# A float32 decoder trunk on one core: S5 output weights staged by two k, four input-matrix buffers, a wide mLSTM gate projection, and two of four state sums left to TensorE

## The chip, the cores and the metric

The kernel runs on one NeuronCore of one Trainium2 chip. Such a core has TensorE (PE in the profile, its weight load PEld), VectorE (DVE), ScalarE (ACT), GpSimd (POOL) and SyncE (SP), whose queue issues most DMAs. Each engine executes its own instructions in the order in which they stand; engines wait for each other by semaphores. The metric is the device time of one execution in microseconds, lower is better. The kernel before takes 1262.76 us, the median of 3 runs (1262.62 to 1263.53).

## What is computed

The reference is a decoder trunk of 4 layers over one sequence of 256 tokens with 1024 channels, in float32. Each layer is a token mixer and a SwiGLU block, both with a residual and a layer norm after:

```python
for i in range(DEPTH):                       # DEPTH = 4
    kind = i % 3                             # 0 HGRN2, 1 mLSTM, 2 S5
    h = mixer[kind](x, ...)
    x = _layernorm(ALPHA * x + h, ln_g[i, 0], ln_b[i, 0])
    x = _layernorm(ALPHA * x + _swiglu(x, ffn_w_gate_up[i], ffn_w_down[i]), ln_g[i, 1], ln_b[i, 1])
```

The change touches the mLSTM mixer (layer 1) at its gates, and the S5 mixer (layer 2):

```python
# mLSTM: 16 gate columns (8 input gates, 8 forget gates) of the input projection
gates = (x @ w_in)[..., 2 * MLSTM_QK_W + 2 * D_MODEL:] + gate_b
# S5: 64 groups of 16 channels, each with a complex diagonal state of 64
u = x @ w_in
bu = einsum('blgc,gpc->blgp', u, bbar)       # complex
s[t] = abar * s[t-1] + bu[t]                 # complex, a scan over the tokens
y = einsum('blgp,gcp->blgc', s_re, c_re) - einsum('blgp,gcp->blgc', s_im, c_im) + d_skip * u
za, zb = split(gelu(y) @ w_out, 2)
return za * sigmoid(zb)
```

## The kernel before

**Two-term products.** Every float32 operand of a large product is held as a high part in float32r (`hi`, `xh`) and the rest (`lo`, `xl`), and a product is three matmuls: high by high, low by high, high by low (`mm3`). Activations lie in one tile `xx` whose two halves are `xh` and `xl`, 256 tokens each.

**Weight stages.** All weights come in stages of 128 partitions by up to 2048 columns (1 MB), in the order of a list (`plan`). `wstage` hands out the next stage and lets `stage_next` prepare the one after (AHEAD = 1). `stage_next` issues a stage's DMA into one of three buffers (tile `w`, line 108), then for each 1024 columns ScalarE makes the high part (line 129) and VectorE the low part (line 130), into one of eight `hi`/`lo` buffer pairs. `as_part` uses such units with tokens as the stationary side, `ws_block` (lines 176 to 182) with weights as the stationary side.

**The order.** The program is traced in the order of the source, and a scheduler at build time then puts each engine's instructions in an order by that priority and by its own idea of what is ready; a NoSync dependency added by hand forces an order on one engine without a semaphore.

**mLSTM gates.** `ml_gw` holds the 16 gate columns in a 128-wide block (8 at column 0, 8 at column 32, the rest zero). Line 713 multiplies it with `ws_block`: 8 slices of k, three matmuls over 256 columns each. Lines 721 and 722 add the gate bias out of PSUM. A chain of operations on 8 partitions follows; it ends in `mr` (line 735), which the first `head` reads on TensorE in line 777, after four `conv` blocks of matmuls.

**S5.** `s5_prepare` builds the tables (rotations `cs`, input matrices `bm`, output matrices `ch`, `cw`) inside the FFNs of layers 0 and 1 and writes them to DRAM (`table_out`). `s5` then runs through four pairs p of blocks, with three rotating working tiles `rot`:

- `project`, `project_part`, `land`: u = x @ w_in by quarters, transposed into place by VectorE
- `inputs(p)` (line 1158): TensorE applies `bm` to u; both blocks of a pair, 128 instructions. `bm` has two buffers, so a pair's matrices can be loaded when the previous `inputs` has read them
- `forth(p)` (lines 1161 to 1174): VectorE rotates the product, adds, and scans along the tokens in chunks of 64 with a real decay
- `back(p)` (lines 1176 to 1183): VectorE rotates the scan's result back: a product `x`, a product `y`, and their sum into the state tile `hs`, 64 values per chunk behind a zero in front (rows of 65)
- `outputs(p)`: TensorE adds the part within a chunk (`cw`, line 1197, 64 matmuls of 64 columns over all pairs) and the part of the state (`ch` by `hs`, line 1204) in PSUM, ScalarE applies GELU. The profile counts each of these float32 matmuls as two instructions: 64 of line 1204 for each pair
- `turn` (lines 1210 to 1219): transposes the result and splits it into `xh` and `xl` for two slices of k
- `few(n)`: takes n of the pieces that `turn` made available. A piece is one pair's share (two slices of k) of one of four output banks (token half h, column half i of `w_out`), 6 matmuls of 512 columns

A stage of `w_so` holds four slices of k for one column half i. So pair 0's four pieces need two stages. Columns 0 to 1023 of the output (n = 0) are made from pieces between the pairs; those of n = 1 follow with `out_part`, and `gated` and the layer norm end the mixer.

## Time and profile before

| | |
|---|---|
| median of 3 runs | 1262.76 us (1262.62 to 1263.53) |
| profiled execution, whole | 1263.76 us |
| its span, first to last instruction | 1262.0 us |
| mean granted TensorE clock | 0.996 |
| DMA over the span | 247.91 MB, 196 GB/s |
| S5 mixer, by the windows shown below | about 640 to 742 us of the span |

The page's first line gives each engine's busy time, its share of the span and its instructions. Matmuls are pipelined: one of 512 columns is busy for 0.40 us, but the next starts 0.23 us after it, so times of a series are read from starts. A number in brackets at the end of an instruction's line is the idle time of its engine ahead of it, with what ended it. The windows are in us from the span's start.

### The profile page before, as it was taken

What the parts mean: (1) busy time and instruction counts of PE and PEld (TensorE: products, weight loads), DVE (VectorE), ACT (ScalarE), POOL (GpSimd) and SP (SyncE); (2) the same over time, 40 slices, a digit from 0 to 9 for tenths busy, and PEclk for the clock granted to TensorE, in tenths of its full rate; (3) what the DMA queues carried; (4) which work ended last, traced back from release to release, by engine and by line L of the source; (5) the groups of instructions that cost most, each with busy time, mean ns of one, the idle gap of its engine ahead of it and who ended that gap; (6) DMA issues with size and microseconds to landing.
All of it is one profiled execution on the core that took longest, in us unless ns stands there. A gap on an engine that the chain in (4) does not pass through costs nothing.

```text
span 1262.0 us, 21505 instructions
## 1 busy us (share of the span) xinstructions
PE 1243.3 (99%) x8541; PEld 1038.9 (82%) x8541; DVE 958.1 (76%) x1703; ACT 704.6 (56%) x1144; POOL 36.2 (3%) x58
## 2 busy tenths in 40 slices
PE   9999999999999999999998999999999999999997
PEld 7977788888798888888886778888889878888886
DVE  6887899876787799866599787666586887766664
ACT  6755576565467555666443455555459654555551
POOL 0000000000100100000000000000000000000000
PEclk9999999999999999999999999999999999999999
DMA  8833466665374266656569546555545432745530
GB/s 310 299 135 134 169 219 230 251 228 200 102 278 148 100 249 237 240 201 224 185 240 337 192 165 248 187 200 179 188 156 217 169 132 95 276 173 194 190 144 34
DMA packets 46340, 247.91 MB, mean 196 GB/s; under 512 B 5504, under 2 KB 11024, under 8 KB 19872
## 3 DMA queue, kind: packets, MB, share of 16 engines
q1 hardware_dynamic: 46112, 246.46, 53.8%
q8 instruction: 67, 1.10, 0.4%
q14 instruction: 33, 0.27, 0.1%
q0 software_dynamic: 128, 0.09, 0.0%
HBM read 233.94 MB, written 12.58 MB: 195 GB/s over the span
## 4 chain that ended last, share of the span: by engine, by line
PE 91%; DVE 4%; DMA 2%; ACT 1%; issue 0%; SPq 0%; DVEq 0%; ACTq 0%
PE g L189 19%; PE g L159 10%; PE g L161 10%; PE g L192 10%; PE g L160 10%; PE a L160 9%; PE a L159 9%; PE a L161 9%; PE a L348 1%; PE t L250 1%; DMA ch<-s5ch 1%; DVE lo L130 1%; PE a L642 1%; DMA first<-in_first 1%; DMA w<-in_w_hg 1%; PE t L1048 1%
## 5 line engine op out<-in xcount | busy, mean ns | idle before, releaser
L130 DVE TENSOR_TENSOR lo<-w,hi 128x1024 fp32r<-128x1024 f32 x389 | 471.8, 1220 | 115.2 <-ACT hi L129 107.9
L129 ACT CAST hi<-w 128x1024 fp32r<-128x1024 f32 x389 | 406.2, 1050 | 201.0 <-PE a L160 112.9
L189 PE MATMUL g<-xx,hi 128*128 128x512 f32 x1024 | 358.2, 395 | 0.0
L192 PE MATMUL g<-xx,lo 128*128 128x256 f32 x1024 | 267.1, 281 | 0.0
L189 PEld LDWEIGHTS g<-xx,hi 128*128 128x128 f32 x1024 | 186.7, 188 | 34.5
L192 PEld LDWEIGHTS g<-xx,lo 128*128 128x128 f32 x1024 | 192.4, 188 | 10.3
L159 PE MATMUL g<-hi,xx 128*128 128x512 f32 (+1 forms) x416 | 167.5, 404 | 2.4 <-ACT xx L269 1.8
L161 PE MATMUL g<-lo,xx 128*128 128x512 f32 (+1 forms) x416 | 165.3, 399 | 0.1
L160 PE MATMUL g<-hi,xx 128*128 128x512 f32 (+1 forms) x416 | 164.7, 397 | 0.0
L329 ACT COPY sum<-g 128x256 f32<-128x256 f32 x128 | 47.6, 372 | 147.7 <-PE g L189 147.5
L159 PE MATMUL a<-hi,hh 128*128 128x512 f32 x328 | 129.4, 395 | 0.0
L161 PE MATMUL a<-lo,hh 128*128 128x512 f32 x328 | 129.2, 394 | 0.0
L160 PE MATMUL a<-hi,hl 128*128 128x512 f32 x328 | 128.8, 393 | 0.0
L330 DVE TENSOR_TENSOR sum<-g,sum 128x256 f32<-128x256 f32 x128 | 54.2, 423 | 69.2 <-ACT sum L329 68.6
L159 PEld LDWEIGHTS g<-hi,xx 128*128 128x128 f32 x416 | 78.3, 188 | 20.6 <-ACT xx L269 2.7
L161 PEld LDWEIGHTS g<-lo,xx 128*128 128x128 f32 x416 | 78.2, 188 | 18.9 <-DVE lo L130 2.1
L160 PEld LDWEIGHTS g<-hi,xx 128*128 128x128 f32 x416 | 78.3, 188 | 15.8
L161 PEld LDWEIGHTS a<-lo,hh 128*128 128x128 f32 x328 | 61.5, 188 | 14.5
L160 PEld LDWEIGHTS a<-hi,hl 128*128 128x128 f32 x328 | 61.5, 188 | 14.4 <-DVE hl L319 0.2
L159 PEld LDWEIGHTS a<-hi,hh 128*128 128x128 f32 x328 | 61.4, 188 | 12.6 <-ACT hh L318 0.2
L159 PE MATMUL g<-xx,hi 128*128 128x256 f32 x200 | 56.4, 282 | 0.9 <-DVE k L593 0.9
L160 PE MATMUL g<-xx,lo 128*128 128x256 f32 x200 | 56.5, 282 | 0.0
(299 smaller groups left out, 1758.0 us busy)
## 6 DMA issues: line engine op xcount, KB each, us to landing
w<-in_w_gu SPq DMA_DIRECT2D x88, 1024.0 KB, 4.8
w<-in_w_dn SPq DMA_DIRECT2D x44, 1024.0 KB, 4.8
w<-in_w_hg SPq DMA_DIRECT2D x30, 1024.0 KB, 5.2
w<-in_w_ml SPq DMA_DIRECT2D x12, 1024.0 KB, 5.1
gb<-in_ln SPq DMA_DIRECT2D x8, 1024.0 KB, 4.8
w<-in_w_ho SPq DMA_DIRECT2D x8, 1024.0 KB, 4.7
w<-in_w_so SPq DMA_DIRECT2D x8, 1024.0 KB, 7.2
s5b<-st SPq DMA_DIRECT2D x16, 256.0 KB, 2.0
```

The source lines that it names most:

```text
L129: self.nc.scalar.copy(hi, x)
L130: self.nc.vector.tensor_tensor(lo, x, hi.bitcast(F32), ALU.subtract)
L159: mm(ps, lh, rh, start=start, stop=False)
L160: mm(ps, ll, rh, start=False, stop=False)
L161: mm(ps, lh, rl, start=False, stop=stop)
L189: whole = lambda: mm(ps, hi[:, c], self.xx[:, k].rearrange("p i t -> p (i t)"), start=k == 0, stop=k == KD - 1)
L192: mm(ps[:, S:], lo[:, c], self.xh[:, k], start=False, stop=False)
L250: nc.tensor.transpose(pt[:, (k % 4) * P : (k % 4 + 1) * P], z[:, k * P : (k + 1) * P], self.ident)
L329: nc.scalar.copy(t, ps[:, S:])
L330: nc.vector.tensor_tensor(t, ps[:, 0:S], t, ALU.add)
L348: nc.tensor.matmul(down[h][n], hidden(h, j, b)[x], dn[j][b][y][:, f], start=False, stop=(x, y, b) == steps[-1])
L642: nc.tensor.matmul(pl[rows(c)].rearrange("p (h a t) -> p a h t", h=2, a=2)[:, i], kk[:, i * P + 32 * c : i * P + 32 * c + 32], view(q, i * ...
```

## The change

- **Gate rows:** `ml_gw` holds the 16 columns twice, at columns 0 and 32 and again at 64 and 96. `stage_next` copies it whole to the high part and then replaces the second copy by the low part (512 elements per partition). One matmul of 512 columns for each k, over `xh` and `xl` together, gives high by both (rows 0 to 39) and low by both (rows 64 to 103). ScalarE and VectorE add the two column halves, ScalarE moves the low rows to partition 0, and two scalar_tensor_tensor add them and the bias.
- **Fetch apart from split:** `fetch` issues a stage's DMA; `stage_next` splits it, and fetches only if that has not been done. `self.behind` is an instruction behind which the low parts of following stages are ordered on VectorE (NoSync).
- **w_so by two k:** a stage holds two slices of k for both column halves, in the order 0, 1, 2, 4, 5, 3, 6, 7; it serves all four pieces of one pair. Splits are called at fixed places after `forth` and after `outputs(3)`, behind the `back` before.
- **Loads:** `bm` has four buffers; `load_in` and `load_out` are called earlier.
- **States:** `hs` is flat, 1 + 1024 values; `table_out` sets the table's value at chunk position 63 to zero, so that the value in front of each chunk is zero. For pairs 1 and 2, `x` and `y` are written to the two `hs` tiles, the sum is left out, and `outputs` issues the state matmuls once for each.

```diff
+TWO = (1, 2)
+    def fetch(self):
+        name, *at = self.plan[self.fetched]
...
+        self.nc.sync.dma_start(st[:, 0 : src.shape[-1]], src)
+        self.landed[self.fetched] = st, src.shape[-1]
+        self.fetched += 1
...
+            elif name == "ml_gw":
+                nc.scalar.copy(hi, part)
+                low = lambda x: x.rearrange("p (k c) -> p k c", k=KD)[:, :, 64:]
+                nc.vector.tensor_tensor(low(hi), low(part), low(hi).bitcast(F32), ALU.subtract)
...
+    def order(self, i, j):
+        if j is not None:
+            dep = mybir.DependencyInfo(mybir.DependencyClass.NoSync, mybir.DependencyReason.DATA)
+            self.tc.add_manual_dep(i, j.name, dep, reason="order")
...
-        self.nc.vector.tensor_tensor(lo, x, hi.bitcast(F32), ALU.subtract)
+        i = self.nc.vector.tensor_tensor(lo, x, hi.bitcast(F32), ALU.subtract).ins
+        self.order(i, self.behind)
...
-            self.ws_block(pz[:, 0:S], self.wstage("ml_gw")[0])
+            gw = self.wstage("ml_gw")[0][0]
+            for k in range(KD):
+                nc.tensor.matmul(pz, gw[:, k * P : (k + 1) * P], self.xx[:, k].rearrange("p i t -> p (i t)"), start=k == 0, stop=k == KD - 1)
...
-            nc.vector.tensor_scalar(li, pz[0:8, 0:S], gbias[:, 0:1], None, ALU.add)
-            nc.vector.tensor_scalar(z, pz[32:40, 0:S], gbias[:, 1:2], None, ALU.add)
+            nc.scalar.copy(sums[0 : 64 + both], pz[0 : 64 + both, S:])
+            nc.vector.tensor_tensor(sums[0 : 64 + both], pz[0 : 64 + both, 0:S], sums[0 : 64 + both], ALU.add)
+            nc.scalar.copy(low, sums[64 : 64 + both])
+            for t, r, i in ((li, 0, 0), (z, 32, 1)):
+                nc.vector.scalar_tensor_tensor(t, sums[r : r + 8], gbias[r : r + 8, i : i + 1], low[r : r + 8], ALU.add, ALU.add)
...
+            nc.gpsimd.memset(cs[:, :, :, 63:64], 0.0)
...
-            key = n, i, k0 // 4
+            key = 4 * n + k0 // 2
             if key not in units:
-                units[key] = self.wstage("w_so", 4 * n + 2 * i + k0 // 4)
-            self.as_part({h: banks[h][i]}, units[key][k0 // 2 % 2 :][:1], k0)
+                units[key] = self.wstage("w_so", key, ahead=0 if key in (0, 1, 2, 4, 5) else AHEAD)
+            self.as_part({h: banks[h][i]}, units[key][i : i + 1], k0)
...
-            hs = [mp.tile([P, 2, 2, 4, 65], F32, name=f"s5hs{i}") for i in range(2)]
+            hs = [mp.tile([P, 1025], F32, name=f"s5hs{i}") for i in range(2)]
...
-                    load(bm, "bm", self.s5_b, b)
+                    load(bm, "bm", self.s5_b, b, 4)
...
+                x, y = map(at, hs) if p in TWO else (x, y)
                 tt(x, g, cs[:, :, 0:1].broadcast_to([P, 2, 2, 256]), ALU.mult)
-                tt(y, g[:, :, ::-1], cs[:, :, 2:0:-1], ALU.mult)
-                tt(h.rearrange("p e r f c -> p (e r f) c")[:, :, 1:], many(x), many(y), ALU.add)
+                i = tt(y, g[:, :, ::-1], cs[:, :, 2:0:-1], ALU.mult)
+                if p not in TWO:
+                    i = tt(hs[p % 2][:, 1:], flat(x), flat(y), ALU.add)
+                return i.ins
...
+                for f, i, h in itertools.product(range(4), range(2), terms):
+                    for g, e in itertools.product(range(2), range(2)):
+                        r, x = slice(64 * g, 64 * g + 64), 64 * (8 * e + 4 * i + f)
+                        last = f == 3 and i == 1 and h is terms[-1]
+                        nc.tensor.matmul(at(g, e, f), h[r, x : x + 64], c[r, i, :, 4 * e + f, :], start=False, stop=last, skip_group_check=True)
```

The sequence of calls in `s5` after the change, from the first pair on (lines that both have are without a sign):

```diff
             inputs(0)
+            load_in(1)
+            self.fetch()
             last = project_part(1, 1, "a")
             forth(0)
             land(last, 8, 1)
-            load_in(1)
             more = project(1, 0, "a")
-            back(0)
+            self.behind = back(0)
+            load_out(1)
+            self.fetch()
             inputs(1)
+            load_in(2)
             outputs(0)
             forth(1)
-            load_out(1)
+            self.stage_next()
+            self.fetch()
             land(more, 16, 0)
             more = project(1, 1, "a", lambda: turn(*todo.pop(0)))
             land(more, 16, 1)
...
             forth(3)
-            load_out(3)
+            self.stage_next()
+            self.fetch()
+            self.fetch()
             few(3)
             turn(*todo.pop(0))
             few(1)
-            back(3)
+            self.behind = back(3)
             few(2)
             outputs(3)
+            self.stage_next()
             few(2)
-
+            self.stage_next()
+            self.behind = None
             first = banks[0]
             banks[0] = [self.bank("g") for _ in range(2)]
-            for k in (0, 2):
-                out_part(1, 0, k)
+            out_part(1, 0, 0)
+            self.stage_next()
+            out_part(1, 0, 2)
```

## The prediction

> **What bounds the kernel now.** I read the page's head first, then the windows of the S5 stage, then its engines in order of time.

> ```profile
> span 1262.0 us, 21505 instructions
> PE 1243.3 (99%) x8541; PEld 1038.9 (82%) x8541; DVE 958.1 (76%) x1703; ACT 704.6 (56%) x1144; POOL 36.2 (3%) x58
> ```

> TensorE (PE) is the bound almost everywhere. So an edit can do two things: change the work that TensorE issues, or take away time in which it waits or runs at a lowered clock. The view by windows, cut at the S5 stage's waits, shows where that time is (columns: window, length, busy time of PE, PEld, DVE, ACT, POOL, granted PE clock, DMA share, GB/s):

> ```profile
> 655.90:661.00 5.10, 5.10 (x145) 4.44 (x144) 5.10 (x8) 0.00 (x0) 0.00 (x0) 1.00 0.55 161
> 661.00:664.40 3.40, 3.40 (x119) 2.73 (x117) 3.37 (x6) 0.17 (x1) 0.00 (x0) 1.00 0.99 361
> 664.40:666.60 2.20, 0.11 (x11) 0.03 (x5) 2.20 (x3) 0.44 (x1) 0.00 (x0) 1.00 0.96 395
> 666.60:671.60 5.00, 5.00 (x117) 3.98 (x117) 4.88 (x7) 1.99 (x2) 0.00 (x0) 0.66 0.79 278
> 671.60:680.70 9.10, 9.10 (x187) 7.41 (x187) 9.06 (x12) 2.51 (x5) 0.00 (x0) 1.00 0.86 295
> 680.70:692.00 11.30, 10.53 (x256) 8.53 (x251) 11.21 (x14) 3.62 (x5) 0.00 (x0) 1.00 0.96 353
> 692.00:694.60 2.60, 0.54 (x9) 0.21 (x5) 2.49 (x3) 1.45 (x2) 0.00 (x0) 0.97 1.04 429
> 694.60:697.00 2.40, 2.40 (x65) 2.28 (x66) 2.39 (x4) 0.88 (x3) 0.00 (x0) 0.50 0.99 420
> 697.00:701.50 4.50, 4.50 (x21) 3.58 (x20) 4.50 (x6) 3.25 (x5) 0.00 (x0) 0.90 0.36 146
> 701.50:707.00 5.50, 4.86 (x25) 3.38 (x25) 5.42 (x7) 2.42 (x3) 0.00 (x0) 1.00 0.51 189
> 707.00:710.20 3.20, 3.20 (x101) 2.61 (x99) 3.20 (x4) 0.77 (x1) 0.00 (x0) 1.00 0.00 0
> 710.20:717.70 7.50, 7.50 (x36) 6.04 (x33) 4.13 (x4) 1.71 (x3) 0.00 (x0) 1.00 0.91 328
> 717.70:720.50 2.80, 2.50 (x12) 1.49 (x10) 1.06 (x1) 2.15 (x2) 0.00 (x0) 1.00 0.60 252
> sum 69.60, PE 63.67 PEld 50.74 DVE 60.64 ACT 23.22 POOL 0.00; mean PE 4.55 PEld 3.62 DVE 4.33 ACT 1.66 POOL 0.00
> ```

> Two things are to be seen. TensorE is idle 69.60 − 63.67 = 5.9 us of this stretch (one more window, to 725.5, belongs to the sum). It also loses clock: 5.0 × 0.34 = 1.7 us after the first long wait, 2.4 × 0.50 + 4.5 × 0.10 = 1.65 us after the second. So **9.3 us** of S5 are recoverable on TensorE. And VectorE (DVE) is nearly without a gap up to 710.2: its busy times there add up to 53.8 of 54.3 us. In this one stage it is the second bound.

> The instructions behind the two long waits, and those around them, from the view in order of time:

> ```profile
> 657.11 1.21 SPq L1117 DMA_DIRECT2D bm<-s5b  x2
> 666.57 0.47 PE L1158 MATMUL g<-s5u,bm 128*32 128x64 f32 x17 [2.09 <-issue]
> 694.58 1.99 PE L1204 MATMUL t<-ch,s5hs 64*64 64x64 f32 x64 [2.06 <-DVE s5hs L1183]
> 709.07 1.16 PE L1204 MATMUL t<-ch,s5hs 64*64 64x64 f32 x64
> 667.02 1.23 DVE L1183 TENSOR_TENSOR s5hs<-s5rot,s5rot 128x1024 f32<-128x1024 f32 x1
> 693.30 1.23 DVE L1183 TENSOR_TENSOR s5hs<-s5rot,s5rot 128x1024 f32<-128x1024 f32 x1
> 706.21 1.21 DVE L130 TENSOR_TENSOR lo<-w,hi 128x1024 fp32r<-128x1024 f32 x1
> 707.35 1.21 DVE L1183 TENSOR_TENSOR s5hs<-s5rot,s5rot 128x1024 f32<-128x1024 f32 x1
> 708.49 5.92 DVE L130 TENSOR_TENSOR lo<-w,hi 128x1024 fp32r<-128x1024 f32 x5
> 719.44 1.06 DVE L1219 TENSOR_TENSOR xx<-t,xx 128x512 fp32r<-128x512 f32 x1 [5.04 <-ACT xx L91]
> ```

> **First wait.** inputs(1) stops 17 matmuls before its end. Pair 1's second `bm` matrix was issued only at about 658, when inputs(0) had freed one of the two buffers, and the DMA share was 0.96 to 0.99 while it was on its way. The profile writes "issue" since the landing is not attributed; that it is this DMA is my reading. **Second wait.** outputs(2) waits for the sum in line 1183.

> **The change, part by part.**

> *Gate rows.* The projection `ml_gw` is 24 matmuls of 256 columns now. The first, the last 512-wide ones ahead of them, and the first after them:

> ```profile
> 360.16 0.39 PE L160 MATMUL g<-hi,xx 128*128 128x512 f32 x1
> 360.39 0.40 PE L161 MATMUL g<-lo,xx 128*128 128x512 f32 x1
> 360.63 0.28 PE L159 MATMUL g<-xx,hi 128*128 128x256 f32 x1
> 363.47 0.28 PE L159 MATMUL g<-xx,hi 128*128 128x256 f32 x1
> 370.86 0.62 DVE L735 TENSOR_TENSOR mr<-num,mr 8x256 fp32r<-8x256 f32 x2
> 387.17 0.34 PE L777 MATMUL a<-mr,sel 128*128 128x384 f32 x1
> ```

> Starts are what counts on a pipelined engine: 24 take 363.47 − 360.63 = 2.84 us, and a 512-wide one takes 0.23. Eight of those are 1.87 us: **−0.95 us**. The added evacuation (a copy and an add over 256 columns, a second copy, and scalar_tensor_tensor in place of tensor_scalar) lengthens the chain to `mr`. Its nearest rows are the FFN's copy and add of the same width:

> ```profile
> L329 ACT COPY sum<-g 128x256 f32<-128x256 f32 x128 | 47.6, 372 | 147.7 <-PE g L189 147.5
> L330 DVE TENSOR_TENSOR sum<-g,sum 128x256 f32<-128x256 f32 x128 | 54.2, 423 | 69.2 <-ACT sum L329 68.6
> ```

> That is 0.37 + 0.42 + 0.37, with handoffs some 1.5 us. `mr` is done at 371.5 and first read at 387.17, so 15 us of convolution matmuls hide it; without that cover it would cost the 1.5. The low half of `ml_gw` shrinks from 1024 to 512 elements, which roughly pays on DVE for the add. I put all this at nothing.

> *Two terms.* For pairs 1 and 2 the sum of line 1183 goes (2 × 1.22 us of DVE), and outputs issues each state matmul twice: 2 × 64 more instructions. At full clock 64 of them take 1.16 us (the row at 709.07; some 1.1 from first start to the next instruction's, since the last one's tail overlaps), at half clock 1.99 (the row at 694.58). So **+2.2 us** of TensorE, up to +4.0.

> [...]

> *Four `bm` buffers and earlier loads.* Pair 1's matrices no longer wait for inputs(0). They are the same bytes, brought forward to a stretch where the DMA engines are full as well. What that can push back is the last `w_si` stage, fetched now behind them:

> ```profile
> 641.00:646.00 5.00, 5.00 (x24) 4.03 (x23) 4.89 (x12) 3.35 (x6) 0.08 (x1) 1.00 0.97 374
> bm<-s5b SPq DMA_DIRECT2D x8, 512.0 KB, 5.5
> cs<-s5cs SPq DMA_DIRECT2D x4, 768.0 KB, 8.0
> 638.14 0.33 SPq L108 DMA_DIRECT2D w<-in_w_si  x1
> 651.38 1.05 ACT L129 CAST hi<-w 128x1024 fp32r<-128x1024 f32 x1 [0.74 <-PE a L160]
> ```

> Two `bm` and one `cs`, 1.8 MB, at the 374 GB/s of that window are 4.8 us; the stage issued at 638 is read at 651, held by a buffer and not by its landing, so 4.8 us later still fits. I take 0, with 0 to +3 as bounds. The first wait then goes whole: **−2.1 − 1.7 = −3.8 us**. What would be late next is pair 0's state at 668.3 on DVE; until then project_part and project(1, 0), inputs(1), the `cw` part and half of project(1, 1) are there to run, so nothing need stop.

> *Stages of two k.* A stage now serves all four pieces of one pair, so pair 0's pieces need one stage (2 low halves) rather than two. More filler is ready while DVE scans. It is this, and the sum that goes, that acts on the second wait and the small ones (0.77 in 680.7:692, 0.64 in 701.5:707, 0.3 near 718): together 5.9 − 2.1 + 1.65 = **−5.5 us** at most.

> *What DVE allows.* back(3) ends at 708.6. Without two sums (2.4) and without the seventh low half inside the scans (706.21; six are left) it ends at 705. The queue there: the halves of two stages now stand behind back(3), then one more stage, then turn(3)'s low part in line 1219. The twelve low halves end at 708.49 + 5.92 − 2.4 = 712, and turn(3)'s at 713, against 720.5 now. So VectorE lets S5 gain at most 7.5 us.

> *Rest.* The two memsets on GpSimd ahead of table_out, the longer gate bias and the NoSync orders cost nothing that TensorE sees: the tables are written a layer ahead. Bounds 0 to 0.3 us.

> **The sum.** −3.8 − 5.5 + 2.2 = −7.1 us in S5, about what VectorE allows. Both limits assume that the order written down at build time fits the real durations; it did not for two waits of 2.1 us now. I leave one such wait, 2.1 us: −5.0. With the gate −0.95: **−6.0 us**. The profiled execution took 1263.76 (span 1262.0 and 1.8 around it), 1.0 above the median; I apply the difference to the median, 1262.76: **1256.8**. With the wait half as long it is 1255.7, with one more like it 1258.9; that is this case's own range.

> **Rivals.** (a) *Only the DMA wait goes.* The second wait moves to another pair, since DVE stays gapless and PE must stand for each state. For it: VectorE's 53.8 of 54.3 us. Against: its chain gets 3.6 us shorter. −3.8 + 2.2 − 0.95 = −2.5: 1260.2. (b) *Everything fits*: −7.1 − 0.95 = −8.0: 1254.7. For it: the filler exists; against: the present order. (c) *The clock does not come back*: small waits remain and keep it lowered, so only the idle time is saved: −5.9 + 2.2 − 0.95 = −4.65: 1258.1. Against: both lowered windows stand right behind the long waits. [...] (d) *Slower: TensorE runs dry at back(3).* Stages 4 and 5 have no low half before 705, and pair 2's pieces need turn(2). If turn(2) is late, TensorE stands through back(3) (3 operations, 3.6 us) and the first half (1.2), and then runs at lowered clock (1.7): +6.5. It decides if the second wait and the small ones stay as well: 6.5 + 2.2 − 3.8 − 0.95 = +4: 1266.7. For it: in the present order these halves fill the time around 706. Against: pair 2's 24 matmuls (5.6 us) fit between turn(2) and back(3).

> **How the numbers follow.** Forecast 0.48, (a) 0.20, (b) 0.12, (c) 0.08, (d) 0.12. A measurement can tell about 0.2% (2.5 us) here, so 1260.2 is the line of "faster". (a) lies on it: 0.07 faster, 0.13 same. Faster 0.48 + 0.12 + 0.08 + 0.07 = 0.75, same 0.13, slower 0.12. The range 1253.5 to 1261.5 holds all but (d), with 1.2 us beyond (b) and (a) for the loads and the half clock of the added matmuls.

> **What would show it.** Right: eight 512-wide gate matmuls; no gap in line 1158; outputs of pairs 1 and 2 with 128 instructions near 2.2 us; granted clock 1.00 in nearly all S5 windows; back(3) about 3.5 us earlier relative to inputs(0). Wrong: a gap of over 2 us ahead of a state matmul, or between turn(2) and out_part(1, …), or VectorE with idle time inside the scans, which would mean that the loads became the bound.

## The result, and the profile after

The changed kernel is slower. Its median is **1270.12 us** (6 runs, 1268.09 to 1271.7), against 1263.14 us (6 runs, 1262.38 to 1264.79) of the kernel before on the same chip: a ratio of 1.0048, 95% interval 1.0038 to 1.0059. The profiled execution took 1270.45 us; its span grew by 6.7 us.

From the page of the kernel after, its head and one of its DMA queues (packets, MB, share of 16 engines):

```profile
span 1268.7 us, 21722 instructions
PE 1245.6 (98%) x8653; PEld 1041.2 (82%) x8653; DVE 955.5 (75%) x1702; ACT 705.8 (56%) x1146; POOL 36.5 (3%) x60
...
q8 instruction: 68, 1.11, 0.4%
```

TensorE has 112 matmuls more (128 for the second terms, 16 fewer for the gates). Its busy time grew only from 1243.3 to 1245.6 us, so most of the 6.7 us is idle time. The waits of TensorE in the S5 mixer, 640 to 742 us (who waited, for what: us in all, times, longest), first of the kernel before:

```profile
PE g L1158 <- issue: 2.1, 1, 2.1
PE t L1204 <- DVE s5hs L1183: 2.1, 1, 2.1
PE a L160 <- DVE xx L1219: 0.6, 1, 0.6
...
PE t L1197 <- DVE xx L1219: 0.4, 1, 0.4
PE t L1204 <- issue: 0.4, 1, 0.4
```

and of the kernel after (line 1187 is inputs now, 1237 the state matmuls, 1252 the low part of turn, 183 a matmul of `project` or of a piece):

```profile
PE t L1237 <- issue: 3.9, 2, 3.2
PE a L183 <- DVE xx L1252: 3.6, 1, 3.6
PE g L1187 <- issue: 1.7, 1, 1.7
PE t L1237 <- DVE s5hs L1213: 1.7, 1, 1.7
```

Two waits of 0.5 and 0.2 us stand in both and are left out. The rest add up to 5.6 us before and to 10.9 us after: **+5.3**. The state matmuls add 2.2, the gates take 0.95 away. The clock costs more too. These windows begin after each of the four long waits, in order of time (columns as in the prediction; the third number from the end is the mean granted clock of the window):

```profile
664.70:669.70 5.00, 5.00 (x108) 4.16 (x109) 5.00 (x8) 2.06 (x4) 0.00 (x0) 1.00 0.70 215
676.80:681.80 5.00, 5.00 (x182) 4.14 (x186) 4.29 (x6) 1.99 (x2) 0.00 (x0) 0.66 0.62 210
685.90:690.90 5.00, 5.00 (x48) 4.03 (x48) 4.90 (x6) 0.66 (x2) 0.00 (x0) 0.66 0.60 206
710.10:715.10 5.00, 5.00 (x42) 3.73 (x42) 3.78 (x4) 1.04 (x1) 0.00 (x0) 0.66 0.92 359
```

Three lowered windows are 3 × 5.0 × 0.34 = 5.1 us, where before lost 3.35: +1.75. Together that is 5.3 + 2.2 − 0.95 + 1.75 = 8.3, against 6.7 measured; the account is good to one or two microseconds, and the idle time is its largest term. Now the places of the waits. From TensorE's instructions in order of time, after:

```profile
664.70 0.30 PE L1187 MATMUL g<-s5u,bm 128*32 128x64 f32 x2 [1.70 <-issue]
...
681.13 1.50 PE L1237 MATMUL t<-ch,s5hs 64*64 64x64 f32 x84
685.87 0.80 PE L1237 MATMUL t<-ch,s5hs 64*64 64x64 f32 x36 [3.24 <-issue]
```

inputs(1), which begins at 661.01, still stops, 2 matmuls before its end instead of 17, although its `bm` matrices are no longer issued behind inputs(0). SyncE's queue, after:

```profile
643.03 1.55 SPq L1146 DMA_DIRECT2D bm<-s5b  x2
```

The two are pair 1's matrices. They were issued 18 us before inputs(1) and had landed by 654.2, 10.0 us after the second issue. And outputs(1) stops in the middle of a run whose operands are all there: pair 1's `ch` had landed at 657.4, and VectorE's last write to the state tiles ended at 678.4. No operand that the trace shows is late at either place. In VectorE's queue at the end of the scans, after:

```profile
693.50 1.18 DVE L1252 TENSOR_TENSOR xx<-t,xx 128x512 fp32r<-128x512 f32 x1 [2.40 <-ACT xx L95]
...
705.58 3.49 DVE L152 TENSOR_TENSOR lo<-w,hi 128x1024 fp32r<-128x1024 f32 x3
708.99 1.05 DVE L1252 TENSOR_TENSOR xx<-t,xx 128x512 fp32r<-128x512 f32 x1
```

turn(2)'s low part (708.99) stands behind three low halves, and TensorE waits 3.6 us for it.

### The profile page after: what moved, and what is told of

The parts are those of the page before. It is cut to its first block, busy times and chain, and to the rows that moved or that the text cites. A ratio compares the mean times of both kernels' runs of the same rounds, so it can differ in the third digit from the quotient of the medians.

```text
span 1268.7 us, 21722 instructions
## 1 busy us (share of the span) xinstructions
PE 1245.6 (98%) x8653; PEld 1041.2 (82%) x8653; DVE 955.5 (75%) x1702; ACT 705.8 (56%) x1146; POOL 36.5 (3%) x60
## 3 DMA queue, kind: packets, MB, share of 16 engines
q8 instruction: 68, 1.11, 0.4%
## 4 chain that ended last, share of the span: by engine, by line
PE 94%; DVE 2%; DMA 1%; ACT 1%; issue 1%; SPq 0%; DVEq 0%; ACTq 0%
PE g L212 19%; PE g L182 10%; PE g L184 10%; PE g L183 10%; PE g L215 10%; PE a L183 9%; PE a L184 9%; PE a L182 9%; PE a L371 1%; PE t L273 1%; PE a L665 1%; DMA first<-in_first 1%; PE t L1077 1%; PE a L545 1%; DMA w<-in_w_hg 1%
## 5 line engine op out<-in xcount | busy, mean ns | idle before, releaser
L215 PE MATMUL g<-xx,lo 128*128 128x256 f32 x1024 | 267.1, 281 | 0.0
L353 DVE TENSOR_TENSOR sum<-g,sum 128x256 f32<-128x256 f32 x128 | 54.1, 422 | 69.2 <-ACT sum L352 68.7
L182 PE MATMUL g<-xx,hi 128*128 128x256 f32 x192 | 54.3, 283 | 0.4 <-DVE k L616 0.4
L184 PE MATMUL g<-xx,hi 128*128 128x256 f32 x192 | 54.2, 282 | 0.0
```

The source lines that it names most:

```text
L182: mm(ps, lh, rh, start=start, stop=False)
L184: mm(ps, lh, rl, start=False, stop=stop)
L215: mm(ps[:, S:], lo[:, c], self.xh[:, k], start=False, stop=False)
L353: nc.vector.tensor_tensor(t, ps[:, 0:S], t, ALU.add)
```

## The experiments

After the result I held this theory: **(F)** the waits marked "issue" are TensorE waiting for its own instructions, which arrive in blocks; **(O)** the order on VectorE, turn(2) behind the low halves, is a cost by itself; **(V)** VectorE's chain bounds S5, so that a wait taken from TensorE comes back as another. The rivals were: the operands' DMA is late (R1), and two terms are dear wherever they stand, or not at all (R2).

### Parts of the change alone

**The gate rows alone** on the kernel before (the rest of this edit is as in the change):

```diff
-            self.ws_block(pz[:, 0:S], self.wstage("ml_gw")[0])
+            gw = self.wstage("ml_gw")[0][0]
+            for k in range(KD):
+                nc.tensor.matmul(pz, gw[:, k * P : (k + 1) * P], self.xx[:, k].rearrange("p i t -> p (i t)"), start=k == 0, stop=k == KD - 1)
...
```

> The kernel before with the wide gate projection alone. Work theory: 8 matmuls of 512 columns in place of 24 of 256, 0.95 us less on TensorE and nothing else, so 0.9 to 1.0 us faster than before (ratio 0.9993). Rival (the longer evacuation chain or the changed build-time order costs something): same or slower than before.

1261.85 us, ratio 0.9990 [0.9981, 0.9999]: a small gain. The source of S5 is untouched, but inputs(1) (line 1167 here, from 661.00 on) now stops elsewhere, 2 matmuls before its end; from the view in order of time:

```profile
665.55 0.42 PE L1167 MATMUL g<-s5u,bm 128*32 128x64 f32 x2 [2.56 <-issue]
```

Before it was after 111 of 128. With 16 matmuls fewer 300 us earlier it is after 126, with two `bm` buffers as before. So the place of this wait is set by a count of instructions and not by a buffer.

**The two terms alone**, with the flat state tiles, on the kernel before:

```diff
+TWO = (1, 2)
...
+                x, y = map(at, hs) if p in TWO else (x, y)
...
+                for f, i, h in itertools.product(range(4), range(2), terms):
```

> The kernel before with the flat state tiles and two terms for pairs 1 and 2 alone; stages and loads as before. Fetch theory (TensorE's instructions come in blocks of about 255 and a block that is used up in 2 to 3 us leaves it standing): the 128 added matmuls and weight loads stand in dense runs, so besides their 2.2 us there is a wait without a releaser of 1 to 3 us in line 1204's matmuls of pair 1 or 2: 1 to 5 us slower than before. Rival (only their work, and VectorE's 2.4 us are saved): between 1 us faster and 2.2 us slower, no such wait in the state matmuls.

1268.43 us, 1.0042 [1.0029, 1.0056]: this part carries most of the loss. TensorE in order of time (line 1211 is the state matmuls):

```profile
684.73 0.93 PE L1211 MATMUL t<-ch,s5hs 64*64 64x64 f32 x49 [2.21 <-issue]
...
699.35 2.95 PE L1211 MATMUL t<-ch,s5hs 64*64 64x64 f32 x102 [2.66 <-issue]
```

Here too a run of ready matmuls breaks off in each of the two doubled pairs. Another cost of the two terms can be ruled out: they take both state tiles for one pair, so that back(2) must wait until outputs(1) has read them. VectorE shows no such wait. Its idle time from 654 to 712 us is 2.7 us ahead of turns and 2.3 us ahead of `forth` in the kernel after, and 1.4, 0.7 and 0.4 us ahead of turns, a low half and a transpose here.

**The change without the two terms:**

```diff
-TWO = (1, 2)
+TWO = ()
```

> The changed kernel with the sum back on VectorE for all four pairs (TWO empty); stages, loads and gate as changed. Fetch theory: the waits of 3.2 and 0.6 us inside the state matmuls of pairs 1 and 2 go, with the lowered clock after them (1.4) and 2.2 us of work: 5 to 7 us faster than the changed kernel, so about as before (1263 to 1265). Rival (operand loads land late because the loads were brought forward): the wait without a releaser stays, 2 us faster than the changed kernel (1268). The wait for turn(2)'s low part (3.6 us) should stay in both.

1262.64 us, 0.9993 [0.9984, 1.0002], 7.5 us less than the whole change by the medians, 6.9 by the ratios: no loss is left, but no gain beyond that of the gates either. Of the waits of TensorE in S5:

```profile
PE t L1237 <- DVE s5hs L1216: 2.5, 1, 2.5
PE g L1187 <- issue: 2.4, 1, 2.4
...
PE a L183 <- DVE xx L1252: 0.6, 1, 0.6
```

The wait in inputs(1) stayed, and a state matmul waits 2.5 us for VectorE. I had expected the wait of 3.6 us for turn(2) to stay as well, and that missed: it is 0.6 us. Without the two terms the scheduler puts turn(2)'s low part at 705.60, between the operations of back(3) and ahead of the low halves. So these 7.5 us are not the waits marked "issue" and the work of the two terms alone; the order on VectorE, which came with the two terms, is in them too.

**Four `bm` buffers alone** on the kernel before:

```diff
-                    load(bm, "bm", self.s5_b, b)
+                    load(bm, "bm", self.s5_b, b, 4)
```

> The kernel before with four buffers for the input matrices and nothing else. By the prediction's step (the wait in inputs(1) is the landing of the second matrix): the wait of 2.1 us goes and the lowered clock after it, 3.8 us faster than before. Fetch theory: the matrices are loaded earlier, yet the wait stays at the same matmul (111 of 128) with 1.5 to 3 us; same as before within 1 us.

1263.44 us, 0.9999 [0.9990, 1.0008]: nothing. Of its waits in S5 (lines as before):

```profile
PE t L1204 <- DVE s5hs L1183: 2.1, 1, 2.1
PE t L1197 <- DVE xx L1219: 1.8, 2, 1.2
PE a L161 <- issue: 0.9, 1, 0.9
```

Pair 1's matrices had landed by 655.0, 8 us before inputs(1) began at 663.10, and TensorE still stops in it after 111 of 128 matmuls. So the matrices are not what it waits for there. The wait is 0.45 us, though, where I had expected 1.5 to 3, and one of 0.9 us stands 127 matmuls earlier, in `project`. Longer waits for VectorE took their place (2.1 and 1.8, before 2.1 and 0.4). This speaks for (V), and it answers the prediction's first step: four buffers were worth nothing.

### What the waits marked "issue" are

**Forty tiny matmuls in the warm-up**, ahead of the first layer, added to the kernel after; one execution first, then a set of them:

```diff
+        for _ in range(40):
+            self.nc.tensor.matmul(ps[:, 0:16], z[:, 0:P], z[:, 0:16], start=True, stop=True)
```

> The changed kernel with 40 tiny matmuls (16 columns) more in the warm-up at the start, hundreds of us before S5, so 40 matmuls and 40 weight loads more ahead of everything. Fetch theory: the borders of the instruction blocks move 40 matmuls forward; the wait in inputs(1) comes after some 86 of its 128 matmuls in place of 126, the one in outputs(1)'s long run of state matmuls after some 44 in place of 84. Rival (operands land late): the waits stay at 126 and 84, where the same operands are first read.

> The changed kernel with 40 tiny matmuls in the warm-up again, now timed, since one look had it at 1265.3 us with the waits at other places. Fetch theory: where the block borders fall decides how long the waits are, so the median stays 2 to 6 us below the changed kernel's 1270.1. Rival (that look was one lucky execution): within 1 us of 1270.

The one execution took 1265.34 us (before 1263.65); the median of the set was 1267.04 us, 1.0031 [1.0018, 1.0043]. The state matmuls (line 1239) in order of time, in the profile of the set:

```profile
680.62 0.92 PE L1239 MATMUL t<-ch,s5hs 64*64 64x64 f32 x44
682.32 1.38 PE L1239 MATMUL t<-ch,s5hs 64*64 64x64 f32 x76 [0.78 <-issue]
...
699.08 0.34 PE L1239 MATMUL t<-ch,s5hs 64*64 64x64 f32 x6 [3.75 <-issue]
```

outputs(1) breaks off after 44 instead of after 84: just the 40 that were put in 680 us earlier. inputs(1) runs through, so the wait that I expected after 86 of its matmuls did not come. But a wait of 3.75 us comes near the end of outputs(2). This is as (F) has it: the waits come at fixed counts of instructions. TensorE's matmuls from the start of the span up to a wait can be counted by windows (third group of numbers: PE busy and its count). Up to the waits in inputs(1) and in outputs(1) of the kernel after:

```profile
0.00:664.65 664.65, 659.94 (x4411) 551.10 (x4411) 532.63 (x1042) 398.40 (x657) 25.75 (x46) 1.00 0.58 212
0.00:685.80 685.80, 676.20 (x4792) 564.18 (x4793) 552.72 (x1067) 404.65 (x665) 25.75 (x46) 1.00 0.59 214
```

and up to the wait in outputs(1) with the 40 matmuls:

```profile
0.00:682.30 682.30, 675.60 (x4792) 565.33 (x4793) 549.99 (x1064) 405.04 (x665) 25.76 (x46) 1.00 0.59 213
```

The count is the same, 4792, though another matmul stands there. Counted so, every wait marked "issue" of over 0.6 us in S5, in all of these kernels (one of 0.8 us in the split version without the order behind the scans has no count here), comes at a border, as I call it: after 4284, 4411, 4792, 4919, 5047 or 5175 matmuls (to within one), which lie 127, 128 or three times 127 apart; there is one exception. That is a wait of 1.5 us ahead of outputs(0)'s state matmuls in the kernel with the 40 (1.2 us in its first execution): TensorE goes on at 665.87, just behind the end of VectorE's sum for pair 0 (665.77). So the mark "issue" alone does not tell. Nor does a border always cost time: in the one execution ahead of the set TensorE passed the one in outputs(1) without a wait.

The size of a block is my estimate from the pages of the profile: before 2 × 8541 matmuls and weight loads beside 67 packets (1.10 MB) of queue q8, whose kind is "instruction", after 2 × 8653 beside 68 (1.11 MB), which is 255 and 254 to a packet of 16 KB. Between two borders 127 or 128 matmuls apart there are 254 or 256 matmuls and weight loads. That the packets hold TensorE's instructions is my reading; no view names their engine. In the kernel after, that queue moved one packet while TensorE stood in outputs(1), from 683.10 on, 2.8 us before it went on; the queue's row in the view of DMA for 682.63 to 685.87 us:

```profile
q8 instruction: 1, 0.02, 2.4%
```

**Twenty of them:** the same edit with `range(20)`.

> The same with 20 tiny matmuls. Fetch theory: the borders lie 20 matmuls earlier than in the changed kernel; the waits come at other matmuls than in the changed kernel and in the one with 40, and the time may be anywhere between 1262 and 1272, but not the sum of the same waits at the same places. Rival (operands): waits at the changed kernel's places (126 of inputs(1), 84 of outputs(1)'s run), 1270.

1269.51 us, 1.0047 [1.0034, 1.0059]. Of its waits in S5:

```profile
PE a L185 <- DVE xx L1254: 5.2, 1, 5.2
PE a L185 <- issue: 1.9, 1, 1.9
```

No state matmul has a wait marked "issue" here, and only one such wait is left, 1.9 us in `project` after 4284 matmuls. Yet the kernel is as slow as the whole change: the wait for turn(2) grew from 3.6 to 5.2 us. So clearing one kind of wait exposed the other here. With the 40 it was the other way round: there the wait for turn(2) is 0.4 us, behind the 3.75 us in outputs(2).

**Fewer loads** after the change: pairs 1 to 3 use pair 0's `cs`, `ch` and `cw`, which leaves out their loads (the outputs of those pairs are computed with pair 0's tables).

```diff
-                load(tables, "cs", self.s5_cs, p)
+                if p:
+                    tables[p] = tables[0]
+                else:
+                    load(tables, "cs", self.s5_cs, p)
...
+                if p:
+                    ch[p], cw[2 * p], cw[2 * p + 1] = ch[0], cw[0], cw[1]
+                    return
```

> The changed kernel with pairs 1 to 3 using pair 0's rotation tables and output matrices, so 5.2 MB of S5's loads are left out; the instructions of TensorE and VectorE are the same in number and kind. Fetch theory with contention (a block's fetch waits behind the operand loads on the DMA engines): the waits without a releaser in inputs(1) and in outputs(1)'s state matmuls shrink from 1.7 and 3.2 us to under 1 and 2. Fetch theory without contention: they stay within 0.5 us of what they are.

One execution: 1266.8 us (before 1263.65). Of its waits, the two marked "issue":

```profile
PE g L1193 <- issue: 1.4, 1, 1.4
PE t L1243 <- issue: 0.7, 1, 0.7
```

Without these loads it is still slower than the kernel before, and inputs(1) (line 1193) still stops, so R1 does not explain the loss as a whole. But 1266.8 lies below all six executions of the change (1268.09 the lowest), and the waits marked "issue" in the state matmuls (line 1243) did shrink, from 3.9 to 0.7. Neither expectation fits both waits: 1.4 us in inputs(1) is not under 1, and 0.7 is not near 3.2. Whether a block comes faster when the DMA engines are freer, one execution doesn't settle.

### What the order on VectorE is worth

**turn(2)'s low part ahead of the low halves** in the kernel after:

```diff
-                tt(ol, src, oh.bitcast(F32), ALU.subtract)
+                i = tt(ol, src, oh.bitcast(F32), ALU.subtract)
+                if k.start == 4:
+                    self.behind = i.ins
...
-            self.behind = back(3)
+            back(3)
```

> The changed kernel with turn(2)'s low part ordered on VectorE right behind back(3), ahead of the three low halves that stand before it now; nothing else. Order theory: TensorE's wait of 3.6 us ahead of pair 2's pieces shrinks to under 0.5 and the lowered clock after it (1.5) goes: 4 to 5 us faster than the changed kernel (1265 to 1266). Rival (VectorE has no room here, the halves are only late elsewhere): a wait for low halves of the n = 1 stages takes its place, under 1.5 us faster.

1265.22 us, 1.0018 [1.0009, 1.0027], 4.9 us less than the whole change by the medians, 3.8 by the ratios. Of its waits in S5:

```profile
PE g L1187 <- issue: 2.3, 1, 2.3
PE t L1237 <- issue: 1.8, 2, 1.3
...
PE a L183 <- DVE xx L1252: 0.9, 1, 0.9
```

The wait for turn(2) went from 3.6 to 0.9, and the clock behind it is not lowered any more:

```profile
705.00:710.00 5.00, 4.06 (x45) 3.01 (x44) 5.00 (x6) 0.79 (x1) 0.00 (x0) 1.00 0.10 16
```

Those are 2.7 + 1.7 = 4.4 us, about the whole gain. (O) stands for the kernel with two terms; without them the scheduler had turn(2) early by itself. The waits marked "issue" are still 4.1 us, against 5.6, and the kernel is still slower than before.

**No dense run twice in a row:** one term, turn's low parts ordered behind the last scan, and half of project(1, 1) between the two blocks of inputs(1):

```diff
-TWO = (1, 2)
+TWO = ()
...
-            inputs(1)
+            inputs(1, (0,))
             load_in(2)
-            outputs(0)
...
-            more = project(1, 1, "a", lambda: turn(*todo.pop(0)))
+            def between():
+                inputs(1, (1,))
+                outputs(0)
...
+                turn(*todo.pop(0))
+            last = project(1, 1, "a", between)
```

> The changed kernel with one term for all pairs, each turn's low part ordered behind the scans on VectorE, and half of project(1, 1) put between the two blocks of inputs(1) on TensorE. Fetch and order theory: the wait in inputs(1) (2.4 us in the one-term kernel) shrinks below 1 with the lowered clock after it (about 2), VectorE's idle 3.8 us before its scans of pair 1 goes: 2 to 5 us faster than the one-term kernel (1262.6), so 1258 to 1261. Rival (VectorE's chain sets the end in any order): within 1 us of the one-term kernel.

1261.76 us, 0.9987 [0.9978, 0.9996], a small gain over the kernel before. Its three longest waits in S5, and VectorE's share (fourth group of numbers) of a window within it:

```profile
PE t L1231 <- DVE xx L1252: 3.2, 1, 3.2
PE a L183 <- DVE xx L1252: 2.0, 1, 2.0
PE t L1237 <- DVE s5hs L1216: 1.5, 1, 1.5
```

```profile
656.00:714.00 58.00, 51.29 (x969) 41.63 (x958) 56.30 (x66) 17.10 (x24) 0.00 (x0) 0.94 0.69 254
```

No wait is marked "issue" any more, and TensorE stands 6.7 us for VectorE, which is busy 56.3 of 58.0 us. My 2 to 5 us below the one-term kernel missed; the rival, within 1 us of it, held. S5 itself got no shorter. inputs(0) and turn(3)'s transposes, in this kernel and then in the kernel before:

```profile
654.83 1.99 PE L1187 MATMUL g<-s5u,bm 128*32 128x64 f32 x128
...
716.81 0.60 PE L1247 MATMUL t<-ident,ys 128*128 128x128 f32 x4
```

```profile
655.95 1.99 PE L1158 MATMUL g<-s5u,bm 128*32 128x64 f32 x128
...
717.70 0.60 PE L1214 MATMUL t<-ident,ys 128*128 128x128 f32 x4
```

62.0 us against 61.75. This bears (V) out: with the waits marked "issue" gone and the sums kept, VectorE fills the stage. That it is the amount of its work and not the order that sets this length is argued from the 56.3 us; it was not tested by itself.

**The same without the order behind the scans:**

```diff
-                self.order(tt(ol, src, oh.bitcast(F32), ALU.subtract).ins, self.scan)
+                tt(ol, src, oh.bitcast(F32), ALU.subtract)
```

> As the kernel with the split inputs, but the turns' low parts free in their order on VectorE again. Theory (with the fetch wait gone, TensorE waits for VectorE's chain, and in the split kernel 3.2 us of it are the PSUM bank that turn(0)'s low part holds behind the scans): that wait of 3.2 us ahead of line 1231 shrinks below 1, VectorE idles instead ahead of turn(0)'s low part by less than the one-term kernel's 3.8: 0 to 2 us faster than the split kernel (1261.8). Rival: VectorE's idle time comes back in full, and it is 1 us slower or more.

1261.86 us, 0.9989 [0.9980, 0.9997]: the same. The scheduler puts turn(0)'s low part behind the scans by itself, and the 3.2 us wait stayed. My expectation that it would fall below 1 us missed.

**Two terms for pair 3 alone**, in the split version:

```diff
-TWO = ()
+TWO = (3,)
```

> The kernel with the split inputs, and two terms for pair 3 alone, where no inputs follow and no operand loads run beside it. Theory (two terms cost where they make a dense run while blocks arrive late; VectorE bounds this stage): VectorE's chain ends 1.2 us earlier, TensorE has 1.1 us more, no wait without a releaser of over 1 us in line 1237: between 1 us faster and the same as the split kernel (1261 to 1262). Rival (two terms cost 2.5 us for each pair wherever they stand, as the 5 us of two pairs suggest): 2 us or more slower than the split kernel (1264).

1262.79 us, 0.9992 [0.9983, 1.0001], the split version being 0.9987. Its only wait marked "issue" in S5 is one of 0.2 us in line 1231.

Here 64 added matmuls cost nothing that these runs can tell, so two terms are not dear wherever they stand (R2); nor are they free, as the kernels with pairs 1 and 2 show. Pair 3 has no run of inputs close by and a lower DMA share (0.00 from 704 to 709 us in the split version; 0.80 and 0.78 around outputs(1) and outputs(2) of the kernel after, 683.07 to 686.95 and 695.55 to 701.91 us); which of the two spares it the runs don't separate.

## Why the prediction was wrong

The forecast was 1256.8 us and the range ended at 1261.5; the time was 1270.12. Step by step:

- **Gate, −0.95: right.** The gate rows alone gave 0.9990, some 1.3 us, and their longer chain stayed covered: in the kernel after, `mr`'s last write starts at 373.8 us and its first reader at 385.8.
- **The first wait, −3.8: wrong, and the cause was misread.** I took it for the landing of `bm` since the DMA share was near 1, and said that this was my reading. The trace of before spoke against it already. Its view of DMA, for the second matrix's issue at 658.00 (KB, us to landing):

```profile
bm<-s5b SPq DMA_DIRECT2D x1, 512.0 KB, 5.3
```

So both matrices were there at 663.3, and TensorE stood from 664.5 to 666.57. Besides, in the kernel's order the first of the 128 matmuls to read the second matrix is the 65th and not the 112th. Four buffers alone gave 0.9999 and the stop stayed after 111; with 16 matmuls fewer far ahead it came after 126. So I read it as a late block of TensorE's instructions, which a buffer does not bring: before, q8 moved a packet from 664.28 on, and TensorE went on 2.3 us later.

- **Two terms, +2.2, at most +4.0: mis-sized.** The work itself is about as large as I put it. Alone the part cost 5.1 us (1268.43 against 1263.34), and within the change 7.5, of which 3.0 are the wait for turn(2). What I had not priced is that 128 matmuls with 128 weight loads are, by the estimate above, a whole block of instructions used up in 2.2 us, and that waits marked "issue" came among them: 2.21 and 2.66 us with the two terms alone, 3.24 and 0.62 us in the whole change.
- **The second wait and the small ones, −5.5 less one wait of 2.1: wrong.** The step treated 9.3 us of idle time and clock as recoverable on TensorE, limited by what VectorE frees. In the kernel after, the waits for VectorE did not go but grew, from 3.1 (2.1, 0.6 and 0.4) to 5.3 us (3.6 and 1.7). In the split version, where no wait marked "issue" is left, 6.7 us of them remain.
- **What VectorE allows, −7.5: its shorter work was right, its use was not.** From forth(0) to back(3), before and after:

```profile
657.70:708.60 50.90, 45.33 (x843) 36.25 (x833) 50.41 (x63) 17.51 (x22) 0.00 (x0) 0.93 0.79 291
```

```profile
655.40:705.70 50.30, 43.07 (x965) 35.18 (x953) 46.46 (x58) 15.10 (x20) 0.00 (x0) 0.93 0.70 259
```

VectorE has 3.95 us less to do (I had said 2.4 + 1.2 for two sums and a low half), but the stretch is only 0.6 us shorter: 3.8 us of it are idle, 0.5 before. The largest piece is the 2.40 us ahead of 693.50 shown above: a turn waits there for the chain that goes through outputs(1), the run that broke off for 3.24 us. That the one follows from the other is my reading. All three signs of being wrong that the prediction names came: a gap of 3.24 us among state matmuls, one of 3.63 us behind turn(2), and idle time on VectorE inside the scans. Its meaning of the third, that the loads became the bound, did not: VectorE's idle time stands ahead of turns and of `forth`, which waits for inputs on TensorE.

- **Rival (d), chance 0.12, 1266.7: the right side and the right place.** turn(2) was late and TensorE stood for it through the first low halves, then ran at a lowered clock, as described. Its price was 3.6 + 1.2 + 1.7; the wait and the clock behind it measured 3.63 + 1.7. The total was still too low, since the waits marked "issue", 5.6 us, lay on top. What I set against it, that pair 2's 24 matmuls would fit between turn(2) and back(3), failed since turn(2)'s low part was itself queued behind back(3).
- **Rival (c): not borne out.** It had the clock stay low between the waits, and it came back to 1.00 (695.55 to 701.91 us). But three waits lowered it instead of two.

What stays open: whether the split order would carry two terms in pairs 1 and 2, which was not tried; why the scheduler puts turn(2) late with two terms; how far ahead a block is requested; and how much the DMA share lengthens its way. The fastest versions found are the split one (0.9987), the same without the order (0.9989) and the gate rows alone (0.9990). All three beat both kernels; the gain over the kernel before is 0.10 to 0.13%, and each interval ends just below 1.

## What to carry to other kernels

A wait marked "issue" in the middle of a run of identical matmuls should be held against the count of instructions before it is put down to a load: here 16 matmuls fewer some 300 us ahead moved one from after 111 matmuls to after 126, and 40 more, 680 us ahead, moved another from after 84 to after 44, with the loads as they were. Moving work from VectorE to TensorE as many short matmuls had a price here beyond its time, 5.1 us for 2.2 us of work in pairs 1 and 2 and none that could be told in pair 3. And idle time on the busiest engine is not yet gain: what ends the waits one step later, here VectorE's chain, says how much of it can be had: in the split version TensorE stood 6.7 us for that chain, with no wait marked "issue" left.

## What the runs showed of the hardware

```profile
704.00:709.00 5.00, 5.00 (x95) 4.06 (x96) 4.97 (x5) 1.53 (x4) 0.00 (x0) 1.00 0.00 0
```

In the kernel before, it was lowered after both long waits (2.09 and 2.06 us), to 0.66 over 5.0 us and to 0.50 over 2.4 us. So in these runs the length of a single wait does not tell, between 1.7 and 2.1 us, whether the clock drops. What else decides was not tried.
